# Linear attention's levels in two groups of four: operands copied out of the state, sixteen 128x64 products per burst

## The chip, the cores and the metric

The kernel runs on one core of a Trainium2 chip. The metric is the time of one execution on the device, in microseconds (us). Engines are named as in the profile: PE is TensorE (PEld its weight loads), DVE is VectorE, ACT is ScalarE, POOL is GpSimd, SP is the engine that issues the DMAs.

## The reference

The reference computes two layers of an encoder on 256 tokens and 16 meta tokens of width 2048. Each layer has one wide input projection, two kinds of attention side by side, an output projection with a layer norm, and a squared-ReLU MLP with a layer norm. The change lies in one of the two attentions, the bidirectional gated linear attention (GLA) with 4 heads of key width 128 and value width 256. For each direction it is the recurrence

```
S = exp(b_last)[..., None] * S + k~^T v          # k~ = k * exp(b_last - cumsum(g))
out = (q * exp(cumsum(g))) S + (masked scores with the decay between two tokens) v
```

The sum of both directions is the same as a 272 x 272 matrix of scores for each head, in which the score of query t and key s is q_t . k_s times, channel by channel, the product of all decays between the two tokens, followed by a product with the values.

## The kernel before, in words

The kernel keeps activations transposed: 128 channels in the partitions, 256 tokens and 16 meta tokens (272 columns) in the free dimension. Everything is bound together by one stream of weights. `made` (L140 to L149) loads a tile of 128 x 1024 weights by DMA (`raw`), ScalarE casts it to a high part `wh` (L147), VectorE takes the difference `wl` (L148), and `by_m` or `by_k` runs the projection products from them (L156, L157, L160 to L162, L186). Two such tiles are kept ready ahead. A tile gives TensorE 24 products of 272 columns in most places. Each product takes a fresh set of weights.

All other work is written as Python generators in two queues, `fg` and `bg`. After each weight tile `pump` runs some steps of both: 1 of `fg` and 1.3 or 1.1 of `bg` while the GLA heads are in it. A step ends at a `yield`. Its instructions then stand in every engine's order at that place, so a head's products stand as short bursts between projection products. The four heads of a layer follow each other in `bg`; heads 2 and 3 run beside the other attention (`na_pair`, neighbourhood attention), whose steps come from `fg`.

A head (`gla_head`, L429 to L545) builds its scores by levels. Level 0 is the diagonal. At level lv two tokens that share a block of 2^lv tokens, but not one of half that size, get their score. For that a state `S` of 128 x 2 x 2 x 272 holds keys and queries (j = 0, 1), for each direction, multiplied by the decays up to the edge of their present block. At each level:

- `gather` (L463 to L467): ScalarE copies the keys of the next level out of `S` into one of two tiles `keys`, alternately from the one direction and from the other, block by block. The queries are not copied; TensorE reads them straight from `S` through `side` (L437), with a stride.
- The products (L485): two of 128 x 128 columns, one for each half of the 256 tokens, so that a level fills 256 columns of a PSUM bank. In layer 0, which computes the meta tokens too (`full`), a product of 16 columns for the meta rows follows at levels 0 to 4 (L488).
- `merge` (L449 to L461): two VectorE products multiply `S` by the decays of the neighbour block, and GpSimd joins the decays themselves.
- The result is taken from PSUM into `A`: at level 0 by ScalarE (L496), then by VectorE's selecting copy with a mask of that level (L498, `copy_predicated`), and for the meta rows into `Am` (L500, L502).

There are levels 0 to 7, each a step of its own, and level 8 between the two halves, copied by ScalarE (L494). Then a step with the meta keys and, in layer 0, the meta queries (L505, L508). After that follow a split of the meta rows (`am`), the products with the values (L523 to L525), their norm, and the gate.

Float32 products, which these are, stand in the trace as two instructions for each product of the program. PSUM has four banks for these bursts (`bank`, the pool `pb`) and four for the projections.

The other attention matters as a neighbour. Its output burst (L633, and L638 in layer 0) writes two heads of 64 channels each, one to PSUM's partitions 0 to 63 and one to 64 to 127.

Of the kernel before, what the change touches and what calls it, by code (L numbers as in the profile page):

```python
# [14 lines left out]
P = 128  # L15
# [32 lines left out]
class Trunk:  # L48
# [18 lines left out]
    def consts(self):  # L67
        nc, c = self.nc, self.cp
        t = lambda n, s, d=F32: c.tile(s, d, name=n, tag=n)
        self.vec = t("vec", [P, DEPTH, 66])  # L70
        nc.sync.dma_start(self.vec, self.i["vec"].rearrange("l p v -> p l v"))
        self.ident = t("ident", [P, P])
        nc.sync.dma_start(self.ident, self.i["ident"])
        self.sel = t("sel", [LRK, 2])
        nc.sync.dma_start(self.sel, self.i["sel"])
        self.qmask = t("qmask", [NM, NK2])
        nc.sync.dma_start(self.qmask, self.i["qmask"])
        self.mask = t("mask", [P, 7, P], U8)
        raw = self.wp.tile([P, WB], F32, name="raw", tag="raw")[:, :7 * P].rearrange("p (l c) -> p l c", l=7)
# [12 lines left out]
        self.one = t("one", [P, 1])  # L92
        nc.gpsimd.memset(self.one, 1.0)
# [129 lines left out]
    def layer(self, l):  # L223
# [4 lines left out]
        with ExitStack() as actx:  # L228
# [36 lines left out]
            with ExitStack() as gctx:  # L265
                self.credit = 0
                self.g2 = pool("gla", "right", gctx, 2)
                self.keys = [self.g2.tile([P, T + P], F32, name=f"keys{i}", tag=f"keys{i}", bufs=1) for i in range(2)]
                for t in self.keys if self.full else ():
                    nc.gpsimd.memset(t[:, L:], 0.0)  # L270
# [158 lines left out]
    def gla_head(self, h):  # L429
        nc, n, full, g2 = self.nc, self.n, self.full, self.g2  # L430
        qk, dec = self.qk[h], self.decay[h]
        A = g2.tile([P, 6, P], F32, name="A", tag="A")
        Am = g2.tile([NM, L], F32, name="Am", tag="Am")
        S = g2.tile([P, 2, 2, L], F32, name="S", tag="S", bufs=1)
        tt = nc.vector.tensor_tensor

        def side(j, lv, start, width):  # L437

            hb = 1 << lv - 1
            return bass.AP(S.tensor, S.offset + j * 2 * L + start,  # L440
                           [S.ap[0], [2 * hb, width // (2 * hb)], [L + hb, 2], [1, hb]])

        def totals(lv, odd, forward, w):

            hb = 1 << lv - 1
            return bass.AP(dec.tensor, dec.offset + (odd + 1) * hb - 1 + (0 if forward else L),
                           [dec.ap[0], [L if forward else -L, 2], [2 * hb, w // (2 * hb)], [0, hb]])

        def merge(lv):  # L449

            hb = 1 << lv - 1
            w = L if lv <= 4 else T
            for odd in (0, 1):
                if lv == 8 and not odd:
                    continue
                o = bass.AP(S.tensor, S.offset + odd * (L + hb),
                            [S.ap[0], [2 * L, 2], [2 * hb, w // (2 * hb)], [1, hb]])
                tt(o, o, totals(lv, 1 - odd, not odd, w), ALU.mult)
            if lv < 8:
                d = [dec[:, :, k * hb - 1:w:2 * hb] for k in (1, 2)]  # L460
                nc.gpsimd.tensor_tensor(d[1], d[1], d[0], ALU.mult)  # L461

        def gather(lv):  # L463
            t = self.keys[lv % 2]
            w = L if full and lv <= 4 else T
            nc.scalar.copy(t[:, :w].rearrange("p (n t h) -> p n t h", t=2, h=1 << lv - 1), side(0, lv, 0, w))
            return t  # L467
# [3 lines left out]
        flat = S.rearrange("p j s c -> p (j s c)")  # L471
        pair = qk.rearrange("p a c -> p (a c)")
        keys = None
        for lv in range(9):
            ps = self.bank()
            p2 = ps[:, :T].rearrange("p (s c) -> p s c", s=2)
            for b in range(2):
                o = ps[:, b * P:b * P + P]
                if lv == 0:
                    k, q = (qk[:, j, b * P:b * P + P] for j in (0, 1))  # L480
                elif lv == 8:
                    k, q = S[:, 0, b, b * P:b * P + P], S[:, 1, 1 - b, P - b * P:T - b * P]
                else:
                    k, q = keys[:, b * P:b * P + P], side(1, lv, b * P, P)
                nc.tensor.matmul(o, lhsT=k, rhs=q, start=True, stop=True)  # L485
            if full and lv <= 4:
                k, q = (keys[:, T:T + P], side(1, lv, T, NM)) if lv else (pair[:, T:T + P], qk[:, 1, T:L])
                nc.tensor.matmul(ps[:, T:L], lhsT=k, rhs=q, start=True, stop=True)  # L488
            if lv:
                merge(lv)  # L490
            if lv < 7:
                keys = gather(lv + 1)
            if lv == 8:
                nc.scalar.copy(A[:, 1:4:2, :], p2)  # L494
            elif lv == 0:
                nc.scalar.mul(A[:, 0:5:4, :], p2, 2.0)  # L496
            else:
                nc.vector.copy_predicated(A[:, 0:5:4, :], self.mask[:, lv - 1:lv, :].to_broadcast([P, 2, P]), p2)  # L498
            if full and lv == 0:
                nc.vector.tensor_scalar(Am[:, T:L], ps[:NM, T:L], 2.0, None, ALU.mult)  # L500
            elif full and lv <= 4:
                nc.vector.copy_predicated(Am[:, T:L], self.mask[:NM, lv - 1, :NM], ps[:NM, T:L])  # L502
            yield
        ps = self.bank()
        nc.tensor.matmul(ps[:, :T], lhsT=flat[:, T:T + P], rhs=S[:, 1, 1, :T], start=True, stop=True)  # L505
        if full:
            for s in range(2):
                nc.tensor.matmul(ps[:, T + s * NM:T + s * NM + NM], lhsT=S[:, 0, 1, s * P:s * P + P],  # L508
                                 rhs=S[:, 1, 0, T:L], start=True, stop=True)
# [3 lines left out]
        am = g2.tile([80, L], F32R, name="am", tag="am")[:, :n]  # L513
# [5 lines left out]
        sq = g2.tile([P, 2, L], F32, name="sq", tag="sq", bufs=1)  # L519
        for e in range(2):  # L520
# [5 lines left out]
            nc.scalar.activation(sq[:, e, :n], o, AF.Square)  # L526
            os_.append(o)
            yield
        nc.vector.tensor_tensor(sq[:, 0, :n], sq[:, 0, :n], sq[:, 1, :n], ALU.add)
        ms = yield from self.mean(sq[:, 0, :n], GDV, pool=g2)  # L530
        rs = g2.tile([P, L], F32, name="grs", tag="grs", bufs=1)[:, :n]
        tn = g2.tile([P, L], F32, name="gtn", tag="gtn", bufs=1)[:, :n]
# [409 lines left out]
def layout(inputs):  # L942
# [58 lines left out]
    xor = p[:, None] ^ p[None]  # L1001
    lev = np.where(xor == 0, 0, np.floor(np.log2(np.maximum(xor, 1))) + 1)
    o["mask"] = np.stack([lev == i + 1 for i in range(7)], axis=1).astype(f)
# [29 lines left out]
```

## Time and profile before

| | us |
|---|---|
| median of three runs | 2420.71 |
| lowest and highest of the three | 2420.54, 2421.34 |
| the profiled execution | 2421.19 |
| its span in the trace | 2419.4 |
| PE busy | 2403.2 |
| DVE busy | 1547.1 |
| ACT busy | 1182.8 |

In the profile's rows, `bg<-S,keys` reads "a tile named bg is written from tiles S and keys", 128*64 after MATMUL is the part of the array in use (128 rows of keys or channels by 64 columns of weights), and `x4` is a number of instructions merged into one row. A group's row gives its busy time and the mean duration of one instruction in ns; what follows the second bar is how long the engine was idle just before such instructions, and who ended that. A timeline row gives the start and the length in us. Matmuls overlap in the array: a product that lasts 0.29 us is followed by the next one 0.126 us later, so the distance of two starts is the price of a product, and not its length. A row of the table by stretches gives the length of the stretch, then busy time and instructions of PE, PEld, DVE, ACT and POOL, the granted TensorE clock, the DMA engines' share and GB/s.

### The profile page before, as it was taken

To read this page: it belongs to the slowest core of one execution; us is meant where nothing else is said; L and a number is where in the kernel's file an instruction comes from. 1 tells how busy PE (TensorE), PEld (TensorE's weight loads), DVE (VectorE), ACT (ScalarE), POOL (GpSimd) and SP (SyncE) were. 2 spreads that over 40 slices of the span, in tenths; PEclk is the share of its full clock that TensorE was granted. 3 is DMA by queue.
4 is the path that set the end of the run, shared out by engine and by line. 5 is a ranking of instruction groups with operands and counts; after the bars stand their busy time and mean duration, and the time that the engine had idled before them with its cause. 6 is when DMAs were issued, how large, how long until landed. Compare 5 with 4: busy or idle time off the path is not lost.

```text
span 2419.4 us, 42868 instructions
## 1 busy us (share of the span) xinstructions
PE 2403.2 (99%) x17326; PEld 2278.6 (94%) x17326; DVE 1547.1 (64%) x2475; ACT 1182.8 (49%) x1972; POOL 120.0 (5%) x206
## 2 busy tenths in 40 slices
PE   9999999999999999999999999999999999999998
PEld 9999999999999999999999899999988888888887
DVE  5587777785544455546576787778866555666655
ACT  6545555564433344444456655555644333444444
POOL 0021110010000000000020011100200000000000
PEclk9999999999999999999999999999999999999999
DMA  7544445555555555555555445446565666665664
GB/s 243 167 140 140 144 137 157 174 175 175 174 175 174 175 175 174 175 175 174 175 177 177 154 150 158 140 154 199 182 186 189 186 190 188 187 186 188 187 188 139
DMA packets 118358, 417.46 MB, mean 173 GB/s; under 512 B 13388, under 2 KB 16332, under 8 KB 118160
## 3 DMA queue, kind: packets, MB, share of 16 engines
q1 hardware_dynamic: 118160, 414.72, 55.2%
q8 instruction: 136, 2.23, 0.4%
q14 instruction: 62, 0.51, 0.1%
HBM read 412.57 MB, written 2.10 MB: 171 GB/s over the span
## 4 chain that ended last, share of the span: by engine, by line
PE 96%; DVE 2%; ACT 1%; issue 1%; DMA 0%; SPq 0%; ACTq 0%; DVEq 0%
PE mm L156 22%; PE mm L160 17%; PE mm L162 17%; PE mm L161 17%; PE mm L157 11%; PE mm L186 6%; PE bg L485 2%; PE bg L633 1%; PE bg L582 1%; DVE wl L148 1%; PE bg L329 0%; PE bg L523 0%; PE bg L618 0%; PE bg L524 0%; DVE acc L852 0%
## 5 line engine op out<-in xcount | busy, mean ns | idle before, releaser
L148 DVE TENSOR_TENSOR wl<-raw,wh 128x1024 fp32r<-128x1024 f32 (+1 forms) x772 | 940.9, 1219 | 701.7 <-ACT wh L147 692.5
L147 ACT CAST wh<-raw 128x1024 fp32r<-128x1024 f32 (+1 forms) x772 | 806.2, 1044 | 1020.4 <-PE mm L161 454.3
L160 PE MATMUL mm<-x,wh 128*128 128x272 f32 (+2 forms) x2176 | 631.7, 290 | 0.0
L162 PE MATMUL mm<-x,wl 128*128 128x272 f32 (+2 forms) x2176 | 628.8, 289 | 0.0
L161 PE MATMUL mm<-x,wh 128*128 128x272 f32 (+2 forms) x2176 | 628.4, 289 | 0.0
L160 PEld LDWEIGHTS mm<-x,wh 128*128 128x128 f32 x2176 | 412.9, 190 | 1.2 <-issue 0.4
L162 PEld LDWEIGHTS mm<-x,wl 128*128 128x128 f32 x2176 | 410.3, 189 | 0.2
L161 PEld LDWEIGHTS mm<-x,wh 128*128 128x128 f32 x2176 | 409.7, 188 | 0.0
L156 PE MATMUL mm<-x,wh 128*128 128x512 f32 x1152 | 409.0, 397 | 0.0
L157 PE MATMUL mm<-x,wl 128*128 128x256 f32 x1152 | 324.7, 282 | 0.0
L156 PEld LDWEIGHTS mm<-x,wh 128*128 128x128 f32 x1152 | 217.5, 189 | 49.8 <-issue 0.4
L156 PE MATMUL mm<-y,wh 128*128 128x512 f32 x688 | 242.1, 393 | 0.0
L157 PEld LDWEIGHTS mm<-x,wl 128*128 128x128 f32 x1152 | 217.4, 189 | 0.1
L162 PE MATMUL mm<-y,wl 128*128 128x272 f32 (+1 forms) x720 | 207.6, 288 | 0.0
L160 PE MATMUL mm<-y,wh 128*128 128x272 f32 (+1 forms) x720 | 207.6, 288 | 0.0
L161 PE MATMUL mm<-y,wh 128*128 128x272 f32 (+1 forms) x720 | 207.2, 288 | 0.0
L157 PE MATMUL mm<-y,wl 128*128 128x256 f32 x688 | 193.0, 281 | 0.6 <-DVE wl L148 0.6
L156 PE MATMUL mm<-u,wh 128*128 128x512 f32 x496 | 174.9, 393 | 0.0
L156 PEld LDWEIGHTS mm<-y,wh 128*128 128x128 f32 x688 | 128.8, 187 | 29.3
L162 PE MATMUL mm<-u,wl 128*128 128x272 f32 (+1 forms) x528 | 152.2, 288 | 0.0
L160 PE MATMUL mm<-u,wh 128*128 128x272 f32 (+1 forms) x528 | 152.2, 288 | 0.0
L161 PE MATMUL mm<-u,wh 128*128 128x272 f32 (+1 forms) x528 | 151.9, 288 | 0.0
(255 smaller groups left out, 3150.8 us busy)
## 6 DMA issues: line engine op xcount, KB each, us to landing
raw<-in_wff SPq DMA_DIRECT2D x512, 512.0 KB, 3.5
raw<-in_win SPq DMA_DIRECT2D x190, 512.0 KB, 3.6
raw<-in_wout SPq DMA_DIRECT2D x64, 512.0 KB, 3.6
nb<-in_nab SPq DMA_DIRECT2D x16, 352.0 KB, 3.4
out<-acc SPq DMA_DIRECT2D x8, 256.0 KB, 2.6
xraw<-in_xT SPq DMA_DIRECT2D x7, 272.0 KB, 5.5
wraw<-in_wup SPq DMA_DIRECT2D x2, 392.0 KB
raw<-in_win SPq DMA_DIRECT2D x4, 128.0 KB, 3.0
```

Source lines behind the costliest of these rows:

```text
L147: nc.scalar.copy(wh[:, c], raw[:, c])
L148: self.wl = nc.vector.tensor_tensor(wl[:, c], raw[:, c], wh[:, c].bitcast(F32), ALU.subtract).ins
L156: mm(ps, lhsT=wh[:, c:c + P], rhs=x.both[:, :, :T], start=first, stop=False)
L157: mm(ps[:, T:], lhsT=wl[:, c:c + P], rhs=xh[:, :T], start=False, stop=last)
L160: mm(o, lhsT=wh[:, c:c + P], rhs=xh[:, :n], start=first, stop=False)
L161: mm(o, lhsT=wh[:, c:c + P], rhs=xl[:, :n], start=False, stop=False)
L162: mm(o, lhsT=wl[:, c:c + P], rhs=xh[:, :n], start=False, stop=last)
L186: self.nc.tensor.matmul(ps[m][:, :n], lhsT=parts[p][0][:, c:c + P], rhs=acts[j][parts[p][1]][:, :n], start=j + p == 0, stop=j == nk - 1 an ...
L485: nc.tensor.matmul(o, lhsT=k, rhs=q, start=True, stop=True)
L582: nc.tensor.matmul(ps[hh][:, t * NKEY:t * NKEY + NKEY], lhsT=q[hs, NM + t * P:NM + t * P + P], rhs=k[hs, t, :], start=True, stop=True)
L633: nc.tensor.matmul(r[hs], lhsT=(v2 if rest else v1)[:, t, hs], rhs=p2[:, t, :] if rest else p1[:, 2 * t + hh, :], start=rest, stop=not rest)
```

## The change

The eight levels 0 to 7 no longer have a burst each. A step now copies and merges only: `gather` copies keys and queries of a level out of `S` into a slot of a new tile `U` (four slots, level modulo 4; at level 1 the queries alone, since its keys are the plain ones), and `merge` follows as before. After levels 1 to 3 have been gathered, `group(0)` makes the products of levels 0 to 3 in one burst, and after 5 to 7 `group(4)` makes those of levels 4 to 7.

Inside a group a level is made of four products of 64 columns of weights by 64 columns, in place of two of 128 by 128. Up to level 6 two tokens that belong together lie in the same 64, so for each 128 tokens (s) the two blocks of 64 (b) go to PSUM's partitions 0 to 63 and 64 to 127; at level 7 the block's queries are those of the other 64. A group fills one bank with 4 x 128 columns. In layer 0 the meta products get a bank of their own, with 64 columns of weights. The masks shrink to 64 columns and six levels. Levels 0 to 6 are selected into a tile `near` of 128 x 2 x 64; at level 7 four small copies, two on ScalarE and two on VectorE, put `near` and level 7 into `A`.

The last level and the meta step become one step. The merge of level 8 goes to a new tile `X` and no longer into `S`, so that the meta products (now two of 128 columns instead of one of 256) read the one half from `S` and the other from `X`. A head has one step fewer. `A`, `Am` and `am` have one buffer instead of two; `sq` is gone and two tiles that exist already take its place; the two `keys` tiles and their clearing are gone.

```diff
-        for lv in range(9):
-            ps = self.bank()
...
-                nc.tensor.matmul(o, lhsT=k, rhs=q, start=True, stop=True)
...
+        def gather(lv):
+
+            w, hb = L if lv <= 4 else T, 1 << lv - 1
+            for j in range(lv == 1, 2):
+                nc.scalar.copy(U[:, lv % 4, j, :w].rearrange("p (n t h) -> p n t h", t=2, h=hb),
+                               bass.AP(S.tensor, S.offset + 2 * j * L,
+                                       [S.ap[0], [2 * hb, w // (2 * hb)], [L + hb, 2], [1, hb]]))
...
+        def group(first):
+
+            ps, pm = self.bank(), self.bank() if full else None
+            for i in range(4):
+                lv = first + i
+                k, q = (qk if lv < 2 else U[:, i])[:, 0], (U[:, i] if lv else qk)[:, 1]
+                for s in range(2):
+                    for b in range(2):
+                        c, r = (s * P + x * 64 for x in (b, b if lv < 7 else 1 - b))
+                        nc.tensor.matmul(ps[b * 64:b * 64 + 64, i * P + s * 64:i * P + s * 64 + 64],
+                                         lhsT=k[:, c:c + 64], rhs=q[:, r:r + 64], start=True, stop=True)
+                if full and lv <= 4:
+                    kq = (qk if lv < 2 else U[:, i]).rearrange("p a c -> p (a c)")
+                    nc.tensor.matmul(pm[:64, i * NM:i * NM + NM], lhsT=kq[:, T:T + 64], rhs=q[:, T:L],
+                                     start=True, stop=True)
+            for i in range(4):
+                lv, p2 = first + i, ps[:, i * P:i * P + P].rearrange("p (s c) -> p s c", s=2)
+                m = pm[:NM, i * NM:i * NM + NM] if full and lv <= 4 else None
+                if lv == 0:
+                    nc.scalar.mul(near, p2, 2.0)
+                    if full:
+                        nc.vector.tensor_scalar(Am[:, T:L], m, 2.0, None, ALU.mult)
+                elif lv == 7:
+                    for b, copy in ((0, nc.scalar.copy), (1, nc.vector.tensor_copy)):
+                        copy(A[half[b], 0:5:4, half[1 - b]], p2[half[b]])
+                        copy(A[half[b], 0:5:4, half[b]], near[half[b]])
+                else:
+                    nc.vector.copy_predicated(near, self.mask[:, lv - 1:lv, :].to_broadcast([P, 2, 64]), p2)
+                    if m is not None:
+                        nc.vector.copy_predicated(Am[:, T:L], self.mask[:NM, lv - 1, :NM], m)
...
+        for lv in range(1, 4):
+            gather(lv)
+            merge(lv)
             yield
+        gather(4)
+        group(0)
+        merge(4)
+        yield
+        for lv in range(5, 8):
+            gather(lv)
+            merge(lv)
+            yield
+        tt(X, blocks(8, 1, T)[:, :, 0, :], totals(8, 1, T)[:, :, 0, :], ALU.mult)
+        group(4)
+        yield
         ps = self.bank()
-        nc.tensor.matmul(ps[:, :T], lhsT=flat[:, T:T + P], rhs=S[:, 1, 1, :T], start=True, stop=True)
+        for b in range(2):
+            nc.tensor.matmul(ps[:, b * P:b * P + P], lhsT=S[:, 0, b, b * P:b * P + P],
+                             rhs=S[:, 1, 1 - b, P - b * P:T - b * P], start=True, stop=True)
+        nc.scalar.copy(A[:, 1:4:2, :], ps[:, :T].rearrange("p (s c) -> p s c", s=2))
+        ps = self.bank()
+        meta = S.rearrange("p j s c -> p (j s c)")[:, T:T + P]
+        for b, q in enumerate((S[:, 1, 1, :P], X[:, 1])):
+            nc.tensor.matmul(ps[:, b * P:b * P + P], lhsT=meta, rhs=q, start=True, stop=True)
         if full:
-            for s in range(2):
-                nc.tensor.matmul(ps[:, T + s * NM:T + s * NM + NM], lhsT=S[:, 0, 1, s * P:s * P + P],
-                                 rhs=S[:, 1, 0, T:L], start=True, stop=True)
+            for b, k in enumerate((S[:, 0, 1, :P], X[:, 0])):
+                nc.tensor.matmul(ps[:, T + b * NM:T + b * NM + NM], lhsT=k, rhs=S[:, 1, 0, T:L], start=True, stop=True)
```

How the instructions move is seen in each engine's order. The first place is TensorE in layer 0, around the output burst of the other attention's first pair, beside which head 2 of the GLA runs. `p`, `v`, `nv` and `pm` are that attention's operands, and `mm` is a projection. Before:

```order
L162 MATMUL mm<-x_389,wl 128x272
L633 MATMUL bg<-p_2712,nv_2132 64x128 x2
L633 MATMUL bg<-p_2711,v_2664 64x128 x2
L633 MATMUL bg<-p_2712,nv_2132 64x128 x2
L633 MATMUL bg<-p_2711,v_2664 64x128 x2
L638 MATMUL bg<-pm,nv_2132 64x16 x2
L485 MATMUL bg<-S,keys_1407 128x128 x2
L488 MATMUL bg<-S,keys_1407 128x16
L160 MATMUL mm<-x_101,wh 128x272
```

And in the changed kernel, from the burst's last products on:

```order
L647 MATMUL bg<-p_2772,v_2718 64x128 x2
L652 MATMUL bg<-pm,nv_2177 64x16 x2
L474 MATMUL bg<-qk_82 64x64 x4
L478 MATMUL bg<-qk_82 64x16
L474 MATMUL bg<-U,qk_82 64x64 x4
L478 MATMUL bg<-U,qk_82 64x16
L474 MATMUL bg<-U 64x64 x4
L478 MATMUL bg<-U 64x16
L474 MATMUL bg<-U 64x64 x4
L478 MATMUL bg<-U 64x16
L160 MATMUL mm<-x_101,wh 128x272
```

Where level 1 stood behind that burst, levels 0 to 3 now stand in one row, directly behind products that also write PSUM's two halves. The same is so for head 3 of layer 0 and for heads 2 and 3 of layer 1.

The second place is TensorE at the end of head 0's scores in layer 0. Before, the meta burst stands alone, 17 projection products behind level 8:

```order
L161 MATMUL mm<-x_389,wh 128x272
L162 MATMUL mm<-x_389,wl 128x272
L505 MATMUL bg<-S 128x256
L508 MATMUL bg<-S 128x16 x2
L160 MATMUL mm<-x_101,wh 128x272
```

Now the second group, the last level and the meta products stand in one row:

```order
L162 MATMUL mm<-x_237,wl 128x272
L474 MATMUL bg<-U 64x64 x4
L478 MATMUL bg<-U 64x16
L474 MATMUL bg<-U 64x64 x12
L516 MATMUL bg<-S 128x128 x2
L522 MATMUL bg<-S 128x128
L522 MATMUL bg<-X,S 128x128
L525 MATMUL bg<-S 128x16
L525 MATMUL bg<-S,X 128x16
L160 MATMUL mm<-x_272,wh 128x272
```

Levels 4 to 7 moved down to the last level there; in the other heads a stretch of projection products or another burst stands between the second group and L516.

The third place is ScalarE in the same head, where `rs` and `rv` are the gate's operands. Before, one copy of keys stands between two weight casts:

```order
L466 COPY keys_1406<-S 128x272
L147 CAST wh<-raw 128x1024
L466 COPY keys_1407<-S 128x272
L147 CAST wh<-raw 128x1024
L405 ACTIVATE rs<-mm 128x272
```

Now up to three, and four a little later:

```order
L147 CAST wh<-raw 128x1024
L452 COPY U<-S 128x272 x3
L402 ACTIVATE rs<-mm 128x272
L405 COPY rv<-mm 128x272
L452 COPY U<-S 128x272
L147 CAST wh<-raw 128x1024
L484 ACTIVATE near<-bg 128x128
```

A step's copies moved ahead of the next weight cast in pairs, and the eviction of level 0 (L484) comes behind a cast of its own.

More of the change, by code (lines that the diff above doesn't have):

```diff
@@ L77, in consts @@
         nc.sync.dma_start(self.qmask, self.i["qmask"])
[L78 to L79 removed]
+        self.mask = t("mask", [P, 6, 64], U8)
+        raw = self.wp.tile([P, WB], F32, name="raw", tag="raw")[:, :6 * 64].rearrange("p (l c) -> p l c", l=6)
         nc.sync.dma_start(raw, self.i["mask"])
@@ L453, in merge @@
             for odd in (0, 1):
[L454 to L467, printed above, removed]
+                o = blocks(lv, odd, w)
@@ new lines, in merge @@
+                tt(o, o, totals(lv, odd, w), ALU.mult)
+            d = [dec[:, :, k * hb - 1:w:2 * hb] for k in (1, 2)]
+            nc.gpsimd.tensor_tensor(d[1], d[1], d[0], ALU.mult)
+        def group(first):
[27 more added lines that the diff above has]
+                        nc.vector.copy_predicated(Am[:, T:L], self.mask[:NM, lv - 1, :NM], m)
@@ L469, in gla_head @@
+        half = [slice(b * 64, b * 64 + 64) for b in range(2)]
         nc.scalar.copy(S[:, 0], qk[:, 0:1, :].to_broadcast([P, 2, L]))
         tt(S[:, 1], dec[:, ::-1, :], qk[:, 1:2, :].to_broadcast([P, 2, L]), ALU.mult)
-        flat = S.rearrange("p j s c -> p (j s c)")
-        pair = qk.rearrange("p a c -> p (a c)")
-        keys = None
-        for lv in range(9):
-            ps = self.bank()
[L476 to L502, printed above, removed]
-            yield
@@ L1000, in layout @@
     o["nab"] = nab.reshape(DEPTH, 8, 4, P, NKEY).transpose(0, 1, 3, 2, 4)
-    xor = p[:, None] ^ p[None]
+    xor = p[:, None] % 64 ^ p[None, :64]
     lev = np.where(xor == 0, 0, np.floor(np.log2(np.maximum(xor, 1))) + 1)
-    o["mask"] = np.stack([lev == i + 1 for i in range(7)], axis=1).astype(f)
+    o["mask"] = np.stack([lev == i + 1 for i in range(6)], axis=1).astype(f)
     o["ident"] = np.eye(P, dtype=f)
```

36 lines of the change are left out of this document (16 added, 20 removed).

## The prediction

> **What bounds the kernel now.** I read the page first: TensorE is busy for nearly the whole span, and the chain that ended last is TensorE's for 96%.
>
> ```profile
> span 2419.4 us, 42868 instructions
> PE 2403.2 (99%) x17326; PEld 2278.6 (94%) x17326; DVE 1547.1 (64%) x2475; ACT 1182.8 (49%) x1972; POOL 120.0 (5%) x206
> PE 96%; DVE 2%; ACT 1%; issue 1%; DMA 0%; SPq 0%; ACTq 0%; DVEq 0%
> ```
>
> Then the table by stretches, for layer 0's attention (115 to 390 us) and for its first GLA head alone:
>
> ```profile
> 115.00:390.00 275.00, 274.27 (x2255) 267.89 (x2255) 205.81 (x458) 144.65 (x342) 38.39 (x70) 1.00 0.45 141
> ...
> 115.22:143.62 28.40, 28.24 (x225) 27.89 (x224) 22.39 (x44) 13.10 (x24) 6.57 (x10) 1.00 0.44 140
> ```
>
> TensorE sat idle for 0.73 of 275 us, at a granted clock of 1.00, while VectorE was busy 75% of the stage, ScalarE 53% and the DMA engines 45%. So this change pays or costs by the time that the level products take on TensorE. A level's products stand as a burst in the stream of projection products, and the timeline gives a burst's price: from the start of the last projection product before it to the start of the second one after it, less two ordinary steps. An ordinary step of a 272-column product is 0.126 us (134.46 to 134.59 below is one).
>
> ```profile
> 115.22 0.29 PE L162 MATMUL mm<-x,wl 128*128 128x272 f32 x1
> 115.34 0.61 PE L485 MATMUL bg<-qk 128*128 128x128 f32 x4
> 115.78 0.29 PE L488 MATMUL bg<-qk 128*128 128x16 f32 x2
> 115.93 0.37 PE L160 MATMUL mm<-x,wh 128*128 128x272 f32 x1
> 116.14 0.29 PE L161 MATMUL mm<-x,wh 128*128 128x272 f32 x1
> ...
> 119.03 0.82 PE L485 MATMUL bg<-S,keys 128*128 128x128 f32 x4
> ...
> 134.46 0.29 PE L161 MATMUL mm<-x,wh 128*128 128x272 f32 x1
> 134.59 0.29 PE L162 MATMUL mm<-x,wl 128*128 128x272 f32 x1
> 134.72 0.61 PE L485 MATMUL bg<-S,keys 128*128 128x128 f32 x4
> 135.08 0.37 PE L160 MATMUL mm<-x,wh 128*128 128x272 f32 x1
> 135.29 0.29 PE L161 MATMUL mm<-x,wh 128*128 128x272 f32 x1
> ...
> 139.39 0.29 PE L160 MATMUL mm<-x,wh 128*128 128x272 f32 x1
> 139.83 0.68 PE L485 MATMUL bg<-S 128*128 128x128 f32 x4 [0.16 <-DVE S L458]
> ...
> 142.37 0.29 PE L162 MATMUL mm<-x,wl 128*128 128x272 f32 x1
> 142.49 0.60 PE L505 MATMUL bg<-S 128*128 128x256 f32 x2
> 142.93 0.51 PE L508 MATMUL bg<-S 128*128 128x16 f32 x4
> 143.29 0.37 PE L160 MATMUL mm<-x,wh 128*128 128x272 f32 x1
> 143.50 0.29 PE L161 MATMUL mm<-x,wh 128*128 128x272 f32 x1
> ```
>
> A float32 product stands as two instructions. A plain level (134.59 to 135.29) costs 0.70 - 0.25 = 0.45 us, that is 4 x 0.112. Level 0 with its meta product costs 0.92 - 0.25 = 0.67, so the meta product alone is 0.22, although it has only 16 columns: its 128-column weight loads set its pace. Level 1 reads its queries out of the state in single elements: its four instructions span 0.82 instead of 0.61, so it costs 0.67 + 0.21 = 0.88. The meta burst at the end costs 1.13 - 0.25 = 0.88. At 139.83 one sees the other kind of loss: 0.44 us after the product before, 0.31 more than a step, waiting for VectorE's merge.
>
> **The change part by part.** *Removed.* A layer-0 head pays for levels 0 to 7: 0.67 + 0.88 + 3 x 0.67 + 3 x 0.45 = 4.91 (level 2, a little dearer, is counted as the others). In layer 1, without meta products, it is 0.45 + 0.66 + 6 x 0.45 = 3.81. The last level and the meta burst are 0.45 + 0.88 = 1.33 in layer 0 and about 0.45 + 0.44 in layer 1. As a check, the window of head 0 holds 225 matmuls, of which 52 are the head's own and two began before it; 28.40 - 171 x 0.126 = 6.85, against 4.91 + 1.33 = 6.24. The 0.61 between them is waits such as the 0.31.
>
> *Added on TensorE.* The nearest thing in the trace to a 64-column product is the neighbourhood attention's output (L633, and L638 with 16 columns), whose two heads write PSUM's two halves:
>
> ```profile
> 313.17 0.24 PE L638 MATMUL bg<-pm,nv 128*64 128x16 f32 x4
> 313.34 0.39 PE L160 MATMUL mm<-x,wh 128*128 128x272 f32 x1
> ...
> 1579.75 0.29 PE L162 MATMUL mm<-x,wl 128*128 128x272 f32 x1
> 1579.97 0.44 PE L633 MATMUL bg<-p,nv 128*64 128x128 f32 x4
> 1580.24 0.39 PE L633 MATMUL bg<-p,v 128*64 128x128 f32 x4
> 1580.46 0.39 PE L633 MATMUL bg<-p,nv 128*64 128x128 f32 x4
> 1580.67 0.39 PE L633 MATMUL bg<-p,v 128*64 128x128 f32 x4
> 1580.99 0.39 PE L160 MATMUL mm<-x,wh 128*128 128x272 f32 x1
> 1581.22 0.29 PE L161 MATMUL mm<-x,wh 128*128 128x272 f32 x1
> ```
>
> From 1580.24 to 1580.67 eight instructions pass in 0.43 us. A full-width product of 128 columns takes 0.112 per instruction, so here two instructions share each 0.108: the halves run side by side. A product of the new kind has 64 columns instead of 128 and half the weights, and I expect its pair to take half, 0.055 to 0.06; I take 0.058. Its bounds are 0.035 (L638's two pairs of 16 columns: 0.17 to the next product, less 0.10 of leaving) and 0.108 (nothing gained from the shorter product). The burst also pays for coming and going: 0.22 instead of 0.126 before the first product, 0.27 instead of 0.217 for the first four, 0.32 instead of 0.217 after the last four, 0.23 instead of 0.126 after that, together 0.345. This is on top of each group, whatever its size.
>
> That halved products cost 0.345 to enter and leave is not so everywhere:
>
> ```profile
> 40.77 0.29 PE L162 MATMUL mm<-x,wl 128*128 128x272 f32 x1
> 40.90 0.67 PE L329 MATMUL bg<-x,ws 128*64 128x272 f32 x4
> ```
>
> L329's 64-column loads follow a full-width product after 0.13 us, an ordinary step; but there a product is one instruction and only one half is used, so L633, with float32 and both halves, is the nearer row. The Trainium skill (TensorEngine Tiling (Array Packing), Key Properties) says that a change of tiling mode drains the engine: by that rule each group pays, as L633 does, and L329's row does not bear it out. With no drain at all the sum below would be 4.1 us better.
>
> A group has 16 products, 32 instructions, 16 pairs: 16 x 0.058 + 0.345 = 1.27. A meta product in it has 16 columns, 64 columns of weights and no partner: half of today's 0.22, so 0.11 (bounds 0.035 and 0.22). Layer 0: the first group has four of them, 1.27 + 0.44 = 1.71, the second one, 1.38; together 3.09 where 4.91 stood, 1.82 saved per head. Layer 1: 2.54 where 3.81 stood, 1.27 saved. The joined burst of last level and meta has eight 128-column instructions and in layer 0 four of 16: 12 x 0.112 = 1.34 and 8 x 0.112 = 0.90, as dear as today's 1.33 and 0.89; a burst of this kind has no entry price that joining could save. Over four heads in each layer: 4 x 1.81 + 4 x 1.26 = 12.3.
>
> *Moved.* In heads 2 and 3 of each layer the first group stands right behind an output burst of the other attention (the order of instructions shows it), so coming and going are shared: up to 4 x 0.345 = 1.4; I take 1.0. And a group reads copies that were made at least one step earlier, so fewer bursts should wait for VectorE or ScalarE as the one at 139.83 did. Eight heads with 0.61 each would be 4.9; the new waits (the X product, the bank for the meta products) take some back. I take 1.5, between 0 and 4.9.
>
> *Beside it.* Four rows show what the other engines give and take:
>
> ```profile
> L148 DVE TENSOR_TENSOR wl<-raw,wh 128x1024 fp32r<-128x1024 f32 x69 | 84.2, 1221 | 46.0 <-ACT wh L147 43.7 <-PE bg L586 2.2
> L458 DVE TENSOR_TENSOR S<-S,dec 128x272 f32<-128x272 f32 x32 | 12.9, 437 | 4.7 <-PE bg L488 4.5
> L498 DVE COPY_PREDICATED A<-mask,bg 128x256 f32<-128x256 uint8 x28 | 12.4, 443 | 0.1
> ...
> L147 ACT CAST wh<-raw 128x1024 fp32r<-128x1024 f32 x70 | 73.3, 1047 | 82.7 <-PE mm L161 61.5 <-issue 11.9 <-PE mm L186 7.7
> L466 ACT COPY keys<-S 128x272 f32<-128x272 f32 x15 | 6.8, 451 | 3.4 <-DVE S L458 3.1
> ```
>
> ScalarE copies 13 tiles a head instead of 7: 6 x 0.45 = 2.7 us, 11 in a layer of 275 us. It is hidden, because ScalarE waited 61.5 us there until TensorE had freed a weight buffer; it is not late. If that cover were gone, the casts behind the copies would hold TensorE up by the same 2.7 a head. VectorE's selecting copies become half as wide and six instead of seven, so at worst 6 x 0.44 instead of 7 x 0.44, less the four small copies of level 7; its merges no longer stand behind TensorE's products (4.5 us of waiting in 32 merges) but behind ScalarE's copies. Queued behind a waiting merge are the weight differences of L148, which themselves waited 43.7 us for ScalarE and have a slack of two tiles. The smaller mask and the two key tiles that need no clearing cost and save nothing on TensorE. The DMA queue loses some bytes of the mask at the start.
>
> The sum is 12.3 + 1.0 + 1.5 = 14.8. The profiled execution took 2421.2 us, its span and 1.8 around it, and is 0.5 above the median of 2420.7: 2421.2 - 14.8 = 2406.4 profiled, 2405.9 against the median.
>
> **The rivals.** *B, the pair does not get shorter.* If each pair keeps its 0.108 (weights not loaded beside the products, or a fixed price per instruction), the 256 pairs cost 256 x 0.05 = 12.8 more and the time is about 2418.7. For it: no row of this trace has 64-wide products of 64 columns, and L638 could be quick only because its few weights had been fetched. Against it: the full-width bursts load 128 columns beside 128 columns of products at 0.112, and half of each should fit in half the time. The Trainium skill (TensorE: Matmul & The Clock Gate, Part 3) says that weight loads overlap running products only where the row groups differ; here all products use all 128 rows, so by it B would come. The trace disagrees: L633's pairs at 0.108 leave no room for a load of their own.
>
> *C, evictions hold a bank.* Today a level gives VectorE one selecting copy per step. The groups hand it up to seven evictions at once: three selecting copies (0.44 at most), two copies of level 7 and up to four of the meta rows, with two merges and X, about 3.5 us, behind up to two weight differences of 1.22: the group's one or two banks of four would be free 5.9 us after it. If the next burst, 24 products or 3.0 us on, needs such a bank, TensorE stands 2.9 us; at all 16 groups that is 46 us and at eight of them 23, which makes the kernel 8 slower: 2429. It decides the sign from 1.2 us per group on. For it: VectorE is the second busiest engine, at 75%. Against: 0.73 us of idle TensorE in 275, and 46.0 us in which VectorE waited before L148.
>
> *D, the change gives less than it says.* Pairs of 0.075 to 0.08, or a dearer entry for short products, cost 4 to 6 us more than the sum: 2411.
>
> **How the numbers follow.** The forecast has 0.77, B 0.08, C 0.05, D 0.10. A difference of 0.2%, 4.8 us, is about what a measurement of this kernel can tell from no change. The forecast and D are both faster by more than that, less a little of their tail: 0.86; B is the same, with that tail: 0.09; C is slower: 0.05. The forecast's own range is 2401 to 2411: pairs of 0.075 (4.4 worse), no drains (4.1 better) or all waits gone (3.4 better). To leave out two in ten at most it reaches to D and half way to B: 2400.5 to 2415.5.
>
> **What would show it.** In the changed profile: the 64x64 instructions of a group, eight of them (four pairs) per 0.23 us in the timeline; 0.22 before the first and 0.32 behind the last; a layer-1 group at 1.3 us and layer-0 groups at 1.7 and 1.4; the joined last burst at 1.34 and 0.90; TensorE idle no more than before in its attention stages. Four pairs per 0.43 would be B. A burst of whatever kind that stands over 1 us behind a VectorE copy out of a group's bank would be C. The forecast is wrong if head 0 of layer 0 costs TensorE more than 5.5 us where it cost 6.85.

## The result and the profile after

The changed kernel takes 2404.73 us (median of four runs, 2404.48 to 2404.93), the kernel before beside it 2421.03 (four runs, 2420.54 to 2421.34). The ratio is 0.9933, with a 95% interval of 0.9916 to 0.995: faster by 16.3 us, where 14.8 were forecast. The profiled execution took 2404.93.

The page's head and its chain, after:

```profile
span 2403.0 us, 43423 instructions
PE 2387.8 (99%) x17598; PEld 2263.4 (94%) x17598; DVE 1545.5 (64%) x2483; ACT 1199.0 (50%) x2036; POOL 127.0 (5%) x204
PE 97%; DVE 2%; issue 1%; ACT 1%; DMA 0%; SPq 0%; POOL 0%; ACTq 0%; DVEq 0%
```

TensorE still sets the end, now with 97% of the chain. It runs 272 matmuls more and is busy 15.4 us less, so those that took the old ones' places are shorter.

Where that lies is read from the two attention stages, each cut from the first product of L329 (L326 after) to the first output projection product (L186). The table by stretches, before:

```profile
40.90:368.69 327.79, 327.27 (x2669) 320.61 (x2667) 232.86 (x489) 179.92 (x402) 37.83 (x70) 1.00 0.47 146
1301.79:1588.03 286.24, 285.51 (x2058) 263.76 (x2056) 216.32 (x417) 171.14 (x376) 30.74 (x71) 1.00 0.49 151
```

And after:

```profile
41.19:358.70 317.51, 317.40 (x2805) 310.99 (x2803) 230.79 (x491) 188.13 (x434) 42.53 (x70) 1.00 0.48 150
1291.80:1571.67 279.87, 279.18 (x2194) 256.66 (x2192) 215.79 (x421) 179.36 (x409) 32.67 (x71) 1.00 0.50 155
```

Layer 0's stage lost 10.28 us and layer 1's 6.37, together 16.65. The first stage starts 0.29 later (41.19 instead of 40.90), and that makes the 16.4 by which the spans differ; the rest of the program stayed. ScalarE has 8.2 us more to do in each stage and VectorE 0.5 to 2.1 less. The granted clock is 1.00 on both sides.

A group in layer 1 after, in the timeline:

```profile
1349.26 0.28 PE L157 MATMUL mm<-x,wl 128*128 128x256 f32 x1
1349.46 0.45 PE L474 MATMUL bg<-qk 128*64 128x64 f32 x8
1349.74 0.40 PE L474 MATMUL bg<-U,qk 128*64 128x64 f32 x8
1349.98 0.64 PE L474 MATMUL bg<-U 128*64 128x64 f32 x16
1350.55 0.50 PE L156 MATMUL mm<-x,wh 128*128 128x512 f32 x1
1350.88 0.28 PE L157 MATMUL mm<-x,wl 128*128 128x256 f32 x1
```

Eight instructions, four pairs, pass in 0.24 us (1349.74 to 1349.98), 0.06 for a pair. The two ordinary steps to be taken off are 0.118 and 0.233 here (256 and 512 columns): 1350.88 - 1349.26 - 0.35 = 1.27 for the burst. Three of layer 1's groups stand alone, and by unrounded starts each of them costs 1.276.

Beside another output burst (head 2 of layer 0, the first place shown in the order) after:

```profile
218.97 0.29 PE L162 MATMUL mm<-x,wl 128*128 128x272 f32 x1
219.19 0.44 PE L647 MATMUL bg<-p,nv 128*64 128x128 f32 x4
...
220.11 0.24 PE L652 MATMUL bg<-pm,nv 128*64 128x16 f32 x4
220.20 0.43 PE L474 MATMUL bg<-qk 128*64 128x64 f32 x8
...
221.91 0.29 PE L161 MATMUL mm<-x,wh 128*128 128x272 f32 x1
```

The joint burst costs 2.94 - 0.25 = 2.69. The two parts alone, elsewhere in the trace, cost 1.295 and 1.697. So 0.30 is paid once instead of twice.

One wait is new. In head 0 of layer 1 after:

```profile
1359.18 1.15 PE L474 MATMUL bg<-U 128*64 128x64 f32 x32
1360.91 0.71 PE L516 MATMUL bg<-S 128*128 128x128 f32 x4 [0.59 <-DVE S L461]
```

Here, as in head 0 of layer 0, the last level stands directly behind the second group (the text on the change named only layer 0), and it waits 0.59 us for VectorE's merge of level 7. The meta product that reads `X` comes late too, and together this head's last products cost 0.88 more than the same products elsewhere. It happens at one of eight heads.

To add the bursts up I took the price of every burst that has two projection products behind it, in the whole program, by the prediction's own measure. Before there were 181 bursts with 141.7 us, after 139 with 125.4: 16.3 less. The other 0.4 of the 16.65 lies in some 3300 ordinary steps, which were 0.1 ns longer each before; the sum is no more exact than that. The experiments are judged by the same sum.

### The profile page after: what moved, and what is told of

Same layout as the page of the kernel before. It is cut to its first block, busy times and chain, and to the rows that moved or that the text cites. A ratio compares the mean times of both kernels' runs of the same rounds, so it can differ in the third digit from the quotient of the medians.

```text
span 2403.0 us, 43423 instructions
## 1 busy us (share of the span) xinstructions
PE 2387.8 (99%) x17598; PEld 2263.4 (94%) x17598; DVE 1545.5 (64%) x2483; ACT 1199.0 (50%) x2036; POOL 127.0 (5%) x204
## 4 chain that ended last, share of the span: by engine, by line
PE 97%; DVE 2%; issue 1%; ACT 1%; DMA 0%; SPq 0%; POOL 0%; ACTq 0%; DVEq 0%
PE mm L156 22%; PE mm L160 18%; PE mm L162 18%; PE mm L161 18%; PE mm L157 11%; PE mm L186 6%; PE bg L647 1%; PE bg L474 1%; DVE wl L148 1%; PE bg L596 1%; PE bg L326 0%; PE bg L539 0%; PE bg L540 0%; PE bg L632 0%; DVE acc L866 0%
```

## The experiments

My theory was the prediction's: halved products that run in pairs give most of it, beside a payment of 0.345 for each burst, a little sharing, and some waits that go. The rivals were B (pairs as dear as a full-width product), a gain from fewer bursts, and a gain from the copied operands or from fewer waits instead of the shorter products.

**e1: do the two halves run beside each other?** The same products, but a group's first half of PSUM is written for all its levels and then the second:

```diff
-            for i in range(4):
-                lv = first + i
-                k, q = (qk if lv < 2 else U[:, i])[:, 0], (U[:, i] if lv else qk)[:, 1]
-                for s in range(2):
-                    for b in range(2):
+            for b in range(2):
+                for i in range(4):
+                    lv = first + i
+                    k, q = (qk if lv < 2 else U[:, i])[:, 0], (U[:, i] if lv else qk)[:, 1]
+                    for s in range(2):
...
```

> The changed kernel with a group's products in another order: all products that write PSUM's partitions 0 to 63 first, then all that write 64 to 127. Same instructions, same number, same bursts. Theory (two halves run side by side; a pair costs 0.058 us): alone, each of a group's 32 instructions takes about 0.056, so a group costs 1.79 + 0.345 = 2.14 where it cost 1.28, and 16 groups 13.8 us more: about 2418.5. Rival (an instruction of 64 columns costs 0.029 whatever half it uses, since it is short and the sequencer is fast): no change, 2404.7.

It took 2415.92 us (2415.51 to 2416.31), a ratio to the kernel before of 0.9979 (0.997 to 0.9988), and 11.2 more than the changed kernel. Its first group in layer 1:

```profile
1355.01 0.28 PE L157 MATMUL mm<-x,wl 128*128 128x256 f32 x1
1355.21 0.45 PE L474 MATMUL bg<-qk 128*64 128x64 f32 x4
1355.49 0.40 PE L474 MATMUL bg<-U,qk 128*64 128x64 f32 x4
1355.73 0.46 PE L474 MATMUL bg<-U 128*64 128x64 f32 x5
...
1357.38 0.28 PE L157 MATMUL mm<-x,wl 128*128 128x256 f32 x1
```

Four instructions take the 0.24 us (1355.49 to 1355.73) that eight took, and the group 2.37 - 0.35 = 2.02. An instruction alone is (2.02 - 0.345) / 32 = 0.052, and a pair 0.058: the second half comes almost free when it stands next to the first. Side by side was right. By prices the order is worth 12.2 us over the 16 groups and not my 13.8, because I had priced the lone instruction above the 0.052 that it takes. The whole time shows 11.2 of it, since the 0.88 around L516 is not paid in this run: the group ahead of it is 0.74 longer, more than the wait of 0.59.

**e2: what does a burst pay for coming and going?** Each group is cut into two bursts:

```diff
             for i in range(4):
+                if i == 2:
+                    yield
...
-        group(0)
+        yield from group(0)
...
-        group(4)
+        yield from group(4)
```

> The changed kernel with a step boundary inside each group, after its second level, so that the products fall into 29 bursts instead of 16 (some stay together), six of them beside an output burst of the other attention instead of four. Theory (each separate burst of halved products pays 0.345 us for coming and going): 23 full payments instead of 12, 3.8 us more: about 2408.5. Rival (the payment belongs to the long output burst alone, or grows with the burst): no more than 1 us more, 2404.7 to 2405.7.

It took 2410.07 us (2409.17 to 2410.27), 0.9955 (0.994 to 0.9969), and 5.3 more than the changed kernel. A half group:

```profile
1361.09 0.28 PE L157 MATMUL mm<-x,wl 128*128 128x256 f32 x1
1361.30 0.69 PE L476 MATMUL bg<-U 128*64 128x64 f32 x16
1361.91 0.50 PE L156 MATMUL mm<-x,wh 128*128 128x512 f32 x1
1362.25 0.28 PE L157 MATMUL mm<-x,wl 128*128 128x256 f32 x1
```

It costs 1.16 - 0.35 = 0.81, which is 8 x 0.058 + 0.345. The payment is as predicted. I had 3.8 for the cuts, and the sum of bursts rose by 5.2. Most of the difference comes from the neighbourhood attention, whose key products fall into two bursts at two places here. (The wait at L516 is gone, which hides some of it.) A key product uses 64 of the rows, so two heads can stand side by side. The first of the two bursts in layer 0, and an uncut burst:

```profile
336.95 0.86 PE L598 MATMUL bg<-nk,nq 64*128 64x176 f32 x4
...
359.84 0.87 PE L598 MATMUL bg<-nk,nq 64*128 64x176 f32 x8
```

Four instructions take the time that eight take. In the uncut burst two of them start 7 ns apart; cut, each stands alone. So half a burst costs as much as a whole one (1.14 against 1.15 in layer 0, 0.99 against 0.99 in layer 1), and the two places cost 2.1 more together. That is e1's effect again, with halves of the rows in place of halves of the columns.

**e3: is it the copied operands?** The kernel before, with the queries of levels 1 and 2 copied too (`A` has one buffer, to make room):

```diff
+            if lv < 3:
+                u = self.queries[lv % 2]
+                nc.scalar.copy(u[:, :w].rearrange("p (n t h) -> p n t h", t=2, h=1 << lv - 1), side(1, lv, 0, w))
...
-                    k, q = keys[:, b * P:b * P + P], side(1, lv, b * P, P)
+                    k, q = keys[:, b * P:b * P + P], self.queries[lv % 2][:, b * P:b * P + P] if lv < 3 else side(1, lv, b * P, P)
```

> The kernel before, in which ScalarE also copies the queries of levels 1 and 2 out of the state, so that TensorE reads them without a stride (A has one buffer instead of two to make room). Nothing else of the change. Theory (a strided read of single elements costs level 1 0.21 us and level 2 0.04): 8 heads x 0.25 = 2.0 us less than before: about 2419.0, and level 1's four instructions stand 0.112 apart instead of 0.164. Rival (the copies' time on ScalarE comes back as waits of TensorE, 16 copies of 0.45): 2421 or more.

It took 2419.07 us (2418.33 to 2419.57), a ratio of 0.9993 with an interval of 0.9983 to 1.0002, which does not by itself separate it from no change, though its slowest run lies below the fastest of the kernel before beside it (2420.24). The trace shows where the time went. Level 1 in it:

```profile
118.93 0.29 PE L162 MATMUL mm<-x,wl 128*128 128x272 f32 x1
119.06 0.60 PE L489 MATMUL bg<-queries,keys 128*128 128x128 f32 x4
...
119.85 0.29 PE L161 MATMUL mm<-x,wh 128*128 128x272 f32 x1
```

The four instructions last 0.60 where the prediction's row has 0.82, and the level costs 0.92 - 0.25 = 0.67 instead of 0.88. Level 2 goes from 0.71 to 0.67. Over eight heads that is 2.0, and the sum of bursts fell by 1.8. That the whole time met the forecast is partly luck, since waits elsewhere came and went. The largest new one is in head 0 of layer 1, where a level waits for ScalarE's copy of its keys, as the rival had it, at one place:

```profile
1362.12 0.71 PE L489 MATMUL bg<-S,keys 128*128 128x128 f32 x4 [0.79 <-ACT keys L467]
```

The copied operands are a real but small part.

**e7: and the halving alone?** The changed kernel with groups of full-width products, two of 128 columns a level, in two banks:

```diff
-                    for b in range(2):
-                        c, r = (s * P + x * 64 for x in (b, b if lv < 7 else 1 - b))
-                        nc.tensor.matmul(ps[b * 64:b * 64 + 64, i * P + s * 64:i * P + s * 64 + 64],
-                                         lhsT=k[:, c:c + 64], rhs=q[:, r:r + 64], start=True, stop=True)
+                    c = s * P
+                    nc.tensor.matmul(ps[:, at + c:at + c + P], lhsT=k[:, c:c + P], rhs=q[:, c:c + P], start=True, stop=True)
...
```

> The changed kernel with its copies, groups and joined last burst, but with full-width products: two of 128 by 128 per level as before the change, in two banks per group, full-width meta products, and the blocks of 64 taken out at the eviction. Theory (the halved, paired products give most of the gain): a group costs 1.79 instead of 1.28 in layer 1, 2.67 and 2.01 instead of 1.70 and 1.39 in layer 0, and the shared payments in four heads go: 4.1 + 6.4 + 1.3 = 11.8 us more, about 2416.5. Rival (the gain comes from copies that TensorE reads without a stride and without waiting, the halving only hides): 2408 or less.

It took 2417.62 us (2416.74 to 2418.3), 0.9986 (0.9977 to 0.9996), 12.9 more than the changed kernel. Its first group in layer 1:

```profile
1356.18 0.28 PE L157 MATMUL mm<-x,wl 128*128 128x256 f32 x1
1356.30 0.61 PE L473 MATMUL bg<-qk 128*128 128x128 f32 x4
1356.75 0.61 PE L473 MATMUL bg<-U,qk 128*128 128x128 f32 x4
...
1358.33 0.28 PE L157 MATMUL mm<-x,wl 128*128 128x256 f32 x1
```

It enters after 0.12, an ordinary step, and pays no 0.345, but 16 instructions at 0.112 make it 2.15 - 0.35 = 1.80 against 1.27. By such prices the halving is worth 10.5 in all, beside the 1.3 of sharing that full-width groups lose. Of the other 1.1, 0.5 are bursts that come late; where the rest lies is open. What is left to this kernel against the one before is 3.3 us: grouping alone, without the halving, is worth little.

**e4: are the waits in the step between copy and use?** The yields after levels 3 and 7 go, so that a group's last copies come right before its products:

```diff
             merge(lv)
-            yield
+            if lv < 3:
+                yield
...
             merge(lv)
-            yield
+            if lv < 7:
+                yield
```

> The changed kernel in which the copies of levels 3 and 7 are made in the group's own step instead of one step earlier; two steps fewer per head. In the order of instructions the groups then fall apart: 30 bursts instead of 16, none beside an output burst. Theory (copies made a step earlier are what took the waits away): 18 more payments of 0.345, 6.2 us, and on top waits before the level whose copies come late, 0.3 us in most of the 16 groups: 2411 to 2416, with gaps of over 0.3 us ahead of single bursts in the timeline. Rival (the waits of the kernel before had another cause): 2411 at most, all from the payments, with no such gaps.

It took 2410.57 us (2409.95 to 2410.82), 0.9957 (0.9942 to 0.9972), 5.8 more than the changed kernel. This was not the test that I wanted: the order put late levels into bursts of their own, a few products further down, and so turned most waits into payments. It has 30 bursts of levels, none beside an output burst, and by the payments alone its bursts would cost 30 x 0.345 - (16 x 0.345 - 1.3) = 6.1 more. Four groups stand directly behind key products, and each pair of bursts costs 0.19 less than its two parts, so 5.4 is left; they cost 5.8 more. The wait at L516 is gone, and two lone levels waited, of which this is one:

```profile
1351.61 0.45 PE L474 MATMUL bg<-U 128*64 128x64 f32 x8 [0.39 <-ACT U L452]
```

The level waits for the copy of its own operands, and its burst costs 1.04 where a lone level costs 0.58. The gaps at many groups that the theory expected are not there, and the run says little on the size of the waits.

**e5: does joining the last level with the meta step save anything?**

```diff
         nc.scalar.copy(A[:, 1:4:2, :], ps[:, :T].rearrange("p (s c) -> p s c", s=2))
+        yield
         ps = self.bank()
```

> The changed kernel with a step boundary between the last level and the meta products, as before the change. In the order of instructions this also moves the groups: 17 bursts, and none of them beside an output burst of the other attention, where four were. Theory (joining the last two bursts saves nothing, a shared payment is worth 0.3): 5 x 0.33 = 1.7 us more, about 2406.4, and the last level 0.45 and the meta burst 0.89 or 0.45 by themselves. Rival (the joint burst saves an exit of its own, 0.2 in each head): 1.6 more on top, 2408.

It took 2405.11 us (2404.84 to 2405.36), 0.9934 (0.992 to 0.9947). In layer 0 the last level alone costs 0.447 and the meta burst 0.894, together 1.341; joined they cost 1.340. Layer 1 has 0.444 + 0.444 against 0.890. Joining saves no TensorE time by itself, as the prediction had it. What the step more does is to move the heads behind it: no group stands at an output burst of the other attention any more, and one is cut in two. The sum of bursts is 1.0 us higher for it, the two attention stages together 0.9, and the median 0.4. The wait at L516 in layer 1 is still there, with the same 0.59.

**e6: one burst for all eight levels.** The groups become one, with more places for the copies, three empty steps ahead, and one payment less for each head:

```diff
-        gather(4)
-        group(0)
-        merge(4)
+        gather(4)
+        merge(4)
...
+        yield
+        yield
+        yield
         tt(X, blocks(8, 1, T)[:, :, 0, :], totals(8, 1, T)[:, :, 0, :], ALU.mult)
-        group(4)
+        group()
```

> The changed kernel with all eight levels in one burst of 32 products: the copies of all levels are kept until then (queries of levels 1 to 4 lent into tiles that are free at that time), three banks per burst in layer 0, three empty steps before it so that it falls well. Eight bursts instead of 16, two of them beside an output burst. Theory (each burst pays 0.345): 6 full payments instead of 12, 2.1 us less: about 2402.6, better than both. Rival (evictions of eight levels at once hold the banks and TensorE waits): 2404.7 or more, with a gap behind such a burst.

It took 2402.44 us (2402.34 to 2402.84), 0.9923 (0.9911 to 0.9936): 2.3 less than the changed kernel, whose lowest run of 2404.48 lies above its highest. A burst of all levels in layer 1:

```profile
1361.84 0.28 PE L157 MATMUL mm<-x,wl 128*128 128x256 f32 x1
1362.05 0.45 PE L487 MATMUL bg<-qk 128*64 128x64 f32 x8
...
1363.26 0.87 PE L487 MATMUL bg<-U 128*64 128x64 f32 x24
...
1364.40 0.28 PE L157 MATMUL mm<-x,wl 128*128 128x256 f32 x1
```

It costs 2.56 - 0.35 = 2.21, which is 32 x 0.058 + 0.345. No burst behind it waits for a bank, though VectorE and ScalarE now get all evictions at once: that speaks against C more strongly than the changed kernel does. The evictions do show one step later: in head 3 of layer 1 the products with the values (L555) wait 0.21 us for VectorE's copy into `A` (L503). It is the fastest version here.

**e8: were there waits before that the idle column does not show?** In the kernel before, a second empty step after each level of head 0, so that a level's merge has twice the time:

```diff
             yield
+            if h == 0:
+                yield
```

> The kernel before with an empty step after each of the levels of head 0 in both layers, so that its copies and merges have twice the time before the next products. Theory (about 0.6 us of head 0's cost in layer 0 are waits for copies and merges): the ten bursts of head 0 in layer 0 cost TensorE 6.2 to 6.3 us instead of 6.85. Rival (the 0.6 is the price of the bursts themselves, not waiting): 6.8 again. The whole time may move either way, since the later heads come later.

Only its trace bears on this; the whole time of its one run, 2424.78 us, does not, since the later heads then come late. Head 0's ten bursts in layer 0 cost 6.27 together, where the kernel before has 6.85. In layer 1 head 0's ten cost 4.65 instead of 5.15. Level 8 of layer 0 in it:

```profile
160.13 0.29 PE L162 MATMUL mm<-x,wl 128*128 128x272 f32 x1
160.25 0.60 PE L485 MATMUL bg<-S 128*128 128x128 f32 x4
...
160.82 0.29 PE L161 MATMUL mm<-x,wh 128*128 128x272 f32 x1
```

It enters after 0.12 and costs 0.69 - 0.25 = 0.44. In the kernel before, whose row at 139.83 the prediction showed, it entered after 0.44 and cost 0.84. So the 0.61 that the prediction found in head 0's window were waits, and head 0 of layer 1 held another 0.5.

## Why the prediction was right

*The pair at 0.058* was read from L633 by halving, and it measured 0.058. The changed kernel, e2 and e6 agree on it for bursts of 8, 16 and 32 pairs. The groups came out at 1.28 in layer 1 (predicted 1.27) and at 1.70 and 1.39 in layer 0 (1.71 and 1.38), the joined last burst at 1.34 and 0.89 (1.34 and 0.90). The meta product was 0.105 (0.11).

*The payment of 0.345* holds, as e2 shows: a half group keeps it whole. This was the place where the rule of a drain (the Trainium skill, TensorEngine Tiling (Array Packing), Key Properties) was weighed against L329's row. The rule fits the groups here: every burst that writes both halves pays, and e7's full-width groups do not. L329's row (0.13, an ordinary step) still does not bear it out.

*The products' part* of the sum was 12.3. By prices it is 10.5 for the halving (e7) and 1.9 for operands that are no longer read in single elements (e3 has 2.0 by prices and 1.8 in the sum of bursts), together 12.4.

*The sharing* was taken at 1.0 of up to 1.4. It is 0.30 twice in layer 0 and 0.35 twice in layer 1, 1.3.

*The waits* are the term that was too small: 1.5 in the sum, about 2.6 measured, which is what is left of the 16.3 after 12.4 and 1.3. They can be found place by place, as the price of a burst above that of the same products where nothing is late. Before, in head 3 of layer 0, where the neighbourhood attention's transposes (L618) come in two pieces:

```profile
284.96 0.29 PE L161 MATMUL mm<-x,wh 128*128 128x272 f32 x1
285.56 0.41 PE L618 MATMUL bg<-ident,ns 128*128 128x128 f32 x2 [0.31 <-DVE nv L610]
...
286.15 0.29 PE L160 MATMUL mm<-x,wh 128*128 128x272 f32 x1
```

Four instructions that cost 0.44 elsewhere cost 1.19 - 0.25 = 0.94. And after, a norm of the gate (L772):

```profile
261.20 0.29 PE L161 MATMUL mm<-x,wh 128*128 128x272 f32 x1
261.59 0.52 PE L772 MATMUL bg<-sp,onesr 128*128 128x272 f32 x2
262.07 0.29 PE L160 MATMUL mm<-x,wh 128*128 128x272 f32 x1
```

It costs 0.87 - 0.25 = 0.62, where such a pair elsewhere costs 0.25; it entered 0.39 after the product before, and the row shows no idle time at all. Summed over both layers' heads (excesses over 0.06):

| excess, us | before | after |
|---|---|---|
| GLA's levels and meta products | 3.3 at 18 places | 0.88 at one head (L516, L522) |
| neighbourhood transposes | 1.03 | 0.32 |
| norms of the gate | 0.25 | 1.05 |

That is 4.6 before and 2.3 after, 2.3 less; a burst of transposes ahead of layer 1's heads (L367 before), which costs 1.35 before and 1.08 after, gives the other 0.3. The step that failed is "Eight heads with 0.61 each would be 4.9; the new waits take some back": the levels held 0.2 to 0.8 a head and 3.3 in all, the new waits of the heads take back 0.9 and 0.8, and the transposes, which I had not counted, gave 0.7 and 0.3. In the changed kernel's attention stages no wait of TensorE that the profile lists is for an eviction out of a bank. That head 0's excess was waiting is shown by e8, which takes away 0.6 in layer 0 and 0.5 in layer 1. For the other places the excess is seen and its cause only argued. The waits of VectorE's merges in layer 0's stage (115 to 390 us) fit it, before:

```profile
DVE S L458 <- PE bg L488: 4.5, 5, 2.2
DVE S L458 <- PE bg L485: 3.0, 3, 1.6
```

And after:

```profile
DVE S L461 <- ACT U L452: 2.6, 4, 0.9
```

Merges waited 7.5 us for TensorE's products and wait 2.6 for ScalarE's copies now. A merge that comes late made the next level's products late, and that chain is cut once products read copies.

*What hides the copies* was ScalarE's spare time, and it did: 8.2 us more of work in a stage, fewer than the 11 that I allowed, and in the two stages TensorE has no listed wait for a weight cast: the only one listed there is the 0.59 at L516.

*The rivals.* B is refuted by the pairs themselves and by e1. Its rule (the Trainium skill, TensorE: Matmul & The Clock Gate, Part 3), that weight loads overlap running products only where row groups differ, does not fit: all rows are in use in each of these products, and a 64-column instruction, its loads included, passes every 0.052 us alone and every 0.029 in pairs. C did not come in the changed kernel, nor in e6. By the prediction's own sum it would have changed the sign from 14.8 / 16 = 0.9 us per group on, not from 1.2. D did not come either: pairs and payment have the size forecast. The prediction would have been wrong with head 0 of layer 0 above 5.5 us; its two bursts of scores cost 4.4.

The predicted 2405.9 is 1.2 above the measured 2404.73. The terms were 1.5 too small together (waits 1.1, sharing 0.3, products 0.1), and the kernel before has a median 0.3 higher here than the one that I started from. The 0.4 in ordinary steps and the first stage's start, 0.3 later, nearly cancel.

## What to carry to other kernels

Where only the two diagonal 64 x 64 blocks of a 128 x 128 float32 product are used, make them two products that write PSUM's two halves, and issue the two next to each other: the order alone was worth 11.2 of 16.3 us here. Such products pay 0.345 us for each burst, so put as many as the operands' storage allows into one (e6), and beside bursts of the same kind. Price a burst from the start before it to the second start after it, since the idle column misses a start that is late while the product before it still lasts.

## What the runs showed of the hardware

A 64-column float32 instruction of 64-column weights takes 0.052 us by itself, and its partner for the other half adds 0.006. Reading a moving operand in single elements costs 0.05 us for each 128-column instruction (0.82 against 0.60 us for four), and copying it first removes that. Products that use half of the rows behave alike: the neighbour's key products, two heads of 64 rows each, take 0.87 us for eight instructions that alternate, and 0.86 for four that stand alone (e2), which I had not put into that run's sum. A group directly behind such key products costs 0.19 less than the two bursts apart (four places in e4).
